# Modulation weights on their own buffers and GpSimd's queue in a hybrid diffusion layer

## The chip, the cores and the metric

The kernel runs on one core of one Trainium2 chip. A core has a matrix engine (TensorE, PE in the profile), a vector engine (VectorE, DVE), an activation engine (ScalarE, ACT), GpSimd (POOL) and SyncE (SP), which here only issues transfers. Sixteen DMA engines move data between the chip's memory (DRAM) and the on-chip buffer. SyncE's transfers form one queue (q1 in the profile), GpSimd's another (q0). The metric is device microseconds of an execution; the time before is the median of three runs.

## What is computed

One layer of a diffusion backbone on 512 latent tokens and 256 context tokens of width 1024, all in float32. Cut to what matters here:

```python
mods = split(silu(c) @ w_mod + b_mod, 9)          # sh1 sc1 g1 sh2 sc2 g2 sh3 sc3 g3, each of 1024
mods_c = split(silu(c_ctx) @ w_mod + b_mod, 9)    # the same for the context tokens
h  = x   + 0.5 * g1  * swiglu(modulate(x,   norm_ffn1, sh1,  sc1),  w_ffn1_in, w_ffn1_out)
hc = ctx + 0.5 * g1c * swiglu(modulate(ctx, norm_ffn1, sh1c, sc1c), w_ffn1_in, w_ffn1_out)
...
h = h + g2 * mixer_output(...)                    # retention and convolution, from h and hc
h = h + 0.5 * g3 * swiglu(modulate(h, norm_ffn2, sh3, sc3), w_ffn2_in, w_ffn2_out)
return rmsnorm(h, final_norm)

def swiglu(x, w_in, w_out):
    a, b = split(x @ w_in, 2)                     # 2 x 2816 columns
    return (silu(a) * b) @ w_out
```

The change lies in the first feed-forward, the two lines with `ffn1`.

## The kernel before

All tensors lie with channels on the 128 partitions and tokens along the row. A float32 product is made of three TensorE products: each operand is split into a rounded part `hi` (a cast on ScalarE) and a rest `lo` (a subtraction on VectorE), and hi x hi, hi x lo and lo x hi are added up in PSUM. So each weight that is loaded goes through DMA, ScalarE and VectorE before TensorE can use it: `unit` (lines 95 to 102) loads into one of four `wraw` buffers through SyncE's queue, casts into one of four `wh` buffers and subtracts into one of four `wl` buffers. `weights` (351 to 357) does the last two steps for weights that are loaded already.

The planner of the language orders the instructions of each engine by their place in the program and by what its model holds to be ready; a load without dependencies may be pulled far forward. Each queue is then served in order. Buffers with one tag are reused in turn, and who needs one waits for its last reader.

`start` (514) loads x and the context, makes the norm and the first shift and scale from the first sixteen blocks of `w_mod` (`first_mods`, 164 to 187, with products on VectorE, ScalarE and, in line 183, GpSimd), and computes two of the 22 column pairs of the feed-forward. At its end it copies x and the context into the DRAM tiles `hdram` and `hcdram` (561, 562).

`ffn1` (424) goes through the 22 column pairs in six groups of 4, 4, 4, 4, 3 and 3 (`GROUPS1`). A group has an input part and an output part. In the first group the pairs 2 and 3 are plain units. All other pairs go through `chunk` (376 to 422), which computes the pair for two quarters of the tokens and weights with seven products in place of eight: `operands` (359) makes sums of tokens once, and `chunk` makes sums of the halves a11, a12, a21, a22 of its weights, into `wy` buffers. Its products are lines 405, 407, 409, 411, 413, 416 and 419 (all matmuls are recorded at line 400), their first Silu is line 410. Its results lie in `sg` buffers.

The output part has four steps (two in the last group and then a tail), each with one load of `w1o` and two blocks of 128 channels for latents (px) and context (pc). For the first five groups `part_sum` (595 to 601) scales each block by its gate on ScalarE into `t` buffers, of which there are six, and adds them to `hdram` and `hcdram` by accumulating stores on GpSimd's queue. The last group loads the sums back (`open_h`, 603 to 613, on SyncE's queue), adds its own block (`evac1`, `evac1c`) and runs the next norm's sums beside it (`tail1`).

Between these parts `mod_step` (568) computes the other 56 blocks of the modulation, in the order of `MOD_STEPS`: `mods` (194 to 204) loads 128 rows of `w_mod` (512 KB) into a `wraw` buffer through SyncE's queue, and VectorE multiplies them by c and, for the first 24, by c_ctx, with the sum kept and the product thrown away into a `t` buffer. Steps 0 to 7 give the gate g1, which `part_sum` needs; it is finished as a whole at step 7. Four steps follow each plain unit, one each chunk and two each output step, until the 56 are used up.

Of the kernel before, what the change touches and what calls it, by code (L numbers as in the profile page):

```python
# [10 lines left out]
F32 = mybir.dt.float32  # L11
# [5 lines left out]
P = 128  # L17
# [7 lines left out]

GROUPS1 = ((0, 4), (4, 4), (8, 4), (12, 4), (16, 3), (19, 3))
LA = L + LC
H = LA // 2
# [24 lines left out]

HOME = {"hx": "right1", "th": "left1", "tl": "left1", "wy": "left1", "sg": "left1"}
HOME.update({t: "left2" for t in ("gx", "gc", "y", "sx", "sc")})
# [4 lines left out]
def hybrid_layer_kernel(ctx: ExitStack, tc: tile.TileContext, a: dict, out: bass.AP):  # L60
# [31 lines left out]
    def raw_tile(shape):  # L92
        return t_(shape, F32, "wraw", 4)
# [100 lines left out]
    def mods(n):  # L194
        i, b = MOD_STEPS[n]
        raw = raw_tile((P, D))
        nc.sync.dma_start(raw, a["w_mod"][n])
        j = 8 * i + b
        for v, dst in ((0, mx), (1, mc)):
            if v == 1 and i > 4:  # L200
                continue
            junk = tmp((P, D), BF16)
            nc.vector.scalar_tensor_tensor(  # L203
                junk, raw, 1.0, ccrow[v], ALU.mult, ALU.mult, accum_out=dst[:, j:j + 1])
# [99 lines left out]
    def part(us, c):  # L304
        return [(hi[:, c], lo[:, c]) for hi, lo in us]
# [53 lines left out]
    def operands(kb):  # L359


        b1, b2 = hx[kb], hx[kb + 4]
        b11, b12, b21, b22 = b1[:, :H], b1[:, H:], b2[:, :H], b2[:, H:]
        ta, tb = t_((P, 2, H), F32, "wy", 2), t_((P, 2, H), F32, "wy", 2)
        nc.vector.tensor_sub(ta[:, 0, :], b11, b12)
        nc.vector.tensor_sub(ta[:, 1, :], b12, b22)
        nc.vector.tensor_sub(tb[:, 0, :], ta[:, 1, :], b11)
        nc.vector.tensor_add(tb[:, 1, :], b21, tb[:, 0, :])
        out = []
        for i, t in enumerate((ta, tb)):  # L370
            hi, lo = t_((P, 2, H), F32R, f"th{2 * kb + i}"), t_((P, 2, H), F32R, f"tl{2 * kb + i}")
            split(hi, lo, t)
            out += [(hi[:, n, :], lo[:, n, :]) for n in range(2)]
        return out

    def chunk(j, u, t):
# [6 lines left out]
        a11, a12, a21, a22 = r0[:, :q], r0[:, q:], r1[:, :q], r1[:, q:]  # L383
        y0, y1 = t_((P, 2, q), F32, "wy", 2), t_((P, 2, q), F32, "wy", 2)
        w0 = weights(r0)
        nc.vector.tensor_add(y0[:, 0, :], a21, a11)
        nc.vector.tensor_add(y0[:, 1, :], a21, a22)
        w1 = weights(y0.rearrange("p a b -> p (a b)"))
        nc.vector.tensor_add(y1[:, 0, :], y0[:, 1, :], a11)
        nc.vector.tensor_add(y1[:, 1, :], y1[:, 0, :], a12)  # L390
        w2 = weights(y1.rearrange("p a b -> p (a b)"))
        w3 = weights(a22)
        lo_, hi_ = slice(0, H), slice(H, LA)
# [9 lines left out]
        p1, p7 = tmp()[:, :H], tmp()[:, :H]  # L403
        s, c = t_((P, LA), F32, "sg", 3), t_((P, LA), F32, "sg", 3)
        product(pa, w0, 0, part(u[:4], lo_), True)
# [4 lines left out]
        nc.scalar.activation(s[:, lo_], pa, AF.Silu)  # L410
        product(pc, w1, 1, [x[0] for x in t], True)
        nc.vector.tensor_sub(p7, p7, pc)
        product(pb, w2, 0, [x[2] for x in t], True)
        nc.vector.tensor_add(p1, p1, pb)
        nc.vector.tensor_sub(c[:, hi_], p7, p1)
        product(pc, w2, 1, part(u[4:], hi_), False)
        nc.vector.tensor_add(s[:, hi_], p1, pc)
        nc.scalar.activation(s[:, hi_], s[:, hi_], AF.Silu)
        product(pd, w3, 0, [x[3] for x in t], False)
        nc.vector.tensor_sub(c[:, lo_], pd, p1)  # L420
        nc.vector.tensor_mul(s, s, c)
        return s

    def ffn1(u):
# [7 lines left out]
        def plain(pa, pb, pc):  # L432
            s = t_((P, LA), F32, "sg", 3)
            nc.scalar.activation(s[:, xs], pa, AF.Silu)
            nc.vector.tensor_mul(s[:, xs], s[:, xs], pb)
            nc.scalar.activation(s[:, cx], pc[:, 0, :], AF.Silu)
            nc.vector.tensor_mul(s[:, cx], s[:, cx], pc[:, 1, :])
            return s
# [6 lines left out]
        off = 0  # L445
        for k0, nk in GROUPS1:
            for j in range(2 if k0 == 0 else 0, nk):
                if k0:
                    keep(j, chunk(k0 + j, u, t))
                    mod_step(1)  # L450
                    continue
                wa, wb = units(a["w1i"][j])
                pa, pb, pc = ps(), ps(), ps((P, 2, LC))
                proj(pa, wa, ux)
                proj(pb, wb, ux)
                proj(pc[:, 0, :], wa, uc)
                proj(pc[:, 1, :], wb, uc)
                keep(j, plain(pa, pb, pc))
                mod_step(4)
            n = 2 * nk * P  # L460
# [8 lines left out]

            for mm in range(2 if last else 4):  # L470
                w = out_units(mm)
                px, pc = [ps() for _ in range(2)], [ps() for _ in range(2)]
# [4 lines left out]
                for i in range(2):  # L477
# [3 lines left out]
                    else:  # L481
                        part_sum(2 * mm + i, px[i], pc[i][:, :LC])
                if not last:
                    mod_step(2)
            if last:
                w = out_units(2) + out_units(3)
                for i in range(4):
                    pc = ps()
                    proj(pc[:, :LC], w[i], gc_)
                    evac1c(hc, 4 + i, pc[:, :LC])  # L490
                mod_step(99)
                px = [ps() for _ in range(4)]
# [21 lines left out]
    def start(u, uc):  # L514
# [45 lines left out]
        nc.gpsimd.dma_start(rope, a["rope"])  # L560
        nc.gpsimd.dma_start(hdram, a["xT"])
        nc.gpsimd.dma_start(hcdram, a["ctxT"])
        return [(px[0], px[1], pc[0]), (px[2], px[3], pc[1])]

    todo = list(range(len(MOD_STEPS)))
    hg = {}

    def mod_step(count):
        for _ in range(count):
            if todo:  # L570
                n = todo.pop(0)
                mods(n)
                if n == 7:
                    hg["x1"] = gate_vec("x1", mx, 2, True)
                    hg["c1"] = gate_vec("c1", mc, 2, True)
                if n == 23:
# [13 lines left out]
    accc = t_((P, LC), F32, "accc")  # L590
    hdram = dp.tile([P, KT, L], F32, name="hdram")

    hcdram = dp.tile([P, KT, LC], F32, name="hcdram")

    def part_sum(b, px, pc):

        r, rc = tmp(), tmp()[:, :LC]
        nc.scalar.activation(r, px, AF.Identity, scale=hg["x1"][:, b:b + 1])
        nc.gpsimd.dma_start(hdram[:, b, :], r, accum_op=ALU.add)
        nc.scalar.activation(rc, pc, AF.Identity, scale=hg["c1"][:, b:b + 1])  # L600
        nc.gpsimd.dma_start(hcdram[:, b, :], rc, accum_op=ALU.add)  # L601

    def open_h():
# [5 lines left out]
        for b in range(KT):  # L609
            nc.sync.dma_start(h[b], hdram[:, b, :])  # L610
        for i in range(4):
            nc.sync.dma_start(hc2[i], hcdram[:, 2 * i:2 * i + 2, :])
        return h, [hc2[b // 2][:, b % 2, :] for b in range(KT)]
# [360 lines left out]
    for b in range(KT):  # L974
        nc.gpsimd.dma_start(h[b], hdram[:, b, :])
    acc = t_((P, L), F32, "acc")
# [164 lines left out]
```

## Time and profile before

| | us |
|---|---|
| median of three runs | 1820.78 (1819.42 to 1824.73) |
| the profiled execution | 1822.34 |
| its span, first to last instruction | 1819.9 |
| TensorE matmuls busy | 1740.2 |
| VectorE busy | 1148.4 |
| ScalarE busy | 673.6 |
| GpSimd busy | 138.3 |
| mean granted clock of TensorE | 0.979 |

The profile records one execution. Its views are the page (busy time of each engine, groups of instructions, the kinds of transfers), windows (busy time of each engine in a stretch that one picks), timelines (instructions of one engine in order: start, length, engine, line, operation, output<-inputs, and in brackets the idle time just before with what ended it) and the DMA view (packets, MB and share of the 16 engines for each queue, in a stretch).

### The profile page before, as it was taken

Reading aid. Unit: us, or ns where it says so; the run is one execution under the profiler, and the core shown is the slowest. Engines: PE = TensorE matmul, PEld = TensorE weight load, DVE = VectorE, ACT = ScalarE, POOL = GpSimd, SP = SyncE. Lnnn points to the kernel's source line nnn. Section 1 sums busy time; section 2 is a strip of 40 time slices with the busy share of each in tenths; the row PEclk is TensorE's granted clock in tenths of the full one; section 3 lists DMA queues with packets and bytes.
Section 4 is the critical chain, followed back from the end, with each engine's and each line's share of the span. In section 5 each row is a group of like instructions: output and inputs, shape, how many; then the busy total and the mean of one; then the engine's idle time right before and its main releaser. Section 6 shows DMA issues by size and latency. Waiting matters only on the chain.

```text
span 1819.9 us, 22626 instructions
## 1 busy us (share of the span) xinstructions
PE 1740.2 (96%) x8918; PEld 1506.7 (83%) x8918; DVE 1148.4 (63%) x1796; ACT 673.6 (37%) x963; POOL 138.3 (8%) x193
## 2 busy tenths in 40 slices
PE   5888999989899789999999999999999999999998
PEld 3677989989899788888888888888888988888887
DVE  5895958566665678877579398474665643333335
ACT  4632434333344532342334234233373332222232
POOL 2303020201121100000000000001010000000000
PEclk8999999999999889999999999999999999999999
DMA  9248475654764513133124115213562233233331
GB/s 325 99 150 180 134 168 169 159 164 125 188 155 94 194 33 104 58 110 122 58 70 168 64 47 174 68 60 128 185 226 99 81 105 93 96 95 99 100 86 46
DMA packets 74062, 221.96 MB, mean 122 GB/s; under 512 B 8818, under 2 KB 14962, under 8 KB 73908
## 3 DMA queue, kind: packets, MB, share of 16 engines
q1 hardware_dynamic: 55444, 179.35, 30.2%
q0 software_dynamic: 17936, 40.13, 9.8%
q8 instruction: 69, 1.13, 0.2%
q10 hardware_dynamic: 576, 1.05, 0.2%
q14 instruction: 37, 0.30, 0.1%
HBM read 192.18 MB, written 31.46 MB: 123 GB/s over the span
## 4 chain that ended last, share of the span: by engine, by line
PE 74%; issue 11%; DVE 6%; DMA 6%; POOL 1%; ACT 1%; DVEq 0%; SPq 0%; POOLq 0%; ACTq 0%
PE ps L108 21%; PE ps L109 21%; PE ps L110 21%; PE ps L400 10%; DMA wraw<-in_w1i 2%; DMA wraw<-in_w1o 1%; DVE wl L101 1%; DMA hx<-in_xT 1%; DVE t L203 1%; DMA wraw<-in_dist_x 1%; DVE h L697 1%; DMA th<-in_w_mod 1%; POOL t L183 1%; POOL hcdram L601 0%; ACT wh L99 0%
## 5 line engine op out<-in xcount | busy, mean ns | idle before, releaser
L99 ACT CAST wh<-wraw 128x1024 fp32r<-128x1024 f32 (+2 forms) x212 | 219.4, 1036 | 557.5 <-PE ps L109 303.9
L101 DVE TENSOR_TENSOR wl<-wraw,wh 128x1024 fp32r<-128x1024 f32 (+2 forms) x212 | 254.3, 1202 | 243.3 <-ACT wh L99 238.2
L108 PE MATMUL ps<-uh,wh 128*128 128x512 f32 (+1 forms) x924 | 333.5, 363 | 8.2 <-ACT wh L99 6.8
L110 PE MATMUL ps<-uh,wl 128*128 128x512 f32 (+1 forms) x924 | 331.6, 360 | 0.9 <-DVE wl L101 0.9
L109 PE MATMUL ps<-ul,wh 128*128 128x512 f32 (+1 forms) x832 | 299.1, 361 | 0.1
L108 PEld LDWEIGHTS ps<-uh,wh 128*128 128x128 f32 x924 | 176.0, 191 | 35.4 <-ACT wh L99 7.2
L109 PE MATMUL ps<-gx,wh 128*128 128x512 f32 (+1 forms) x544 | 204.0, 377 | 0.0
L110 PE MATMUL ps<-gx,wl 128*128 128x512 f32 (+1 forms) x544 | 204.0, 377 | 0.0
L108 PE MATMUL ps<-gx,wh 128*128 128x512 f32 (+1 forms) x544 | 203.7, 377 | 0.2 <-ACT gx L297 0.2
L110 PEld LDWEIGHTS ps<-uh,wl 128*128 128x128 f32 x924 | 175.9, 191 | 27.2 <-DVE wl L101 1.7
L697 DVE SCALAR_TENSOR_TENSOR h<-y,vec,h 128x512 f32<-128x512 f32 x240 | 179.6, 748 | 5.5
L109 PEld LDWEIGHTS ps<-ul,wh 128*128 128x128 f32 x832 | 158.7, 191 | 24.3 <-DVE ul L511 0.9
L108 PE MATMUL ps<-hx,wh 128*128 128x512 f32 (+1 forms) x364 | 124.2, 341 | 10.4 <-DVE gx L587 6.0
L110 PE MATMUL ps<-hx,wl 128*128 128x512 f32 (+1 forms) x364 | 123.6, 340 | 1.1 <-DVE wl L101 1.1
L109 PE MATMUL ps<-hx,wh 128*128 128x512 f32 (+1 forms) x364 | 123.4, 339 | 0.0
L108 PEld LDWEIGHTS ps<-gx,wh 128*128 128x128 f32 x544 | 102.1, 188 | 18.9 <-ACT gx L297 0.4
L110 PEld LDWEIGHTS ps<-gx,wl 128*128 128x128 f32 x544 | 102.0, 188 | 18.8
L109 PEld LDWEIGHTS ps<-gx,wh 128*128 128x128 f32 x544 | 102.0, 188 | 18.7
L400 PE MATMUL ps<-th,wh 128*128 128x384 f32 x288 | 97.5, 339 | 4.0 <-ACT wh L355 3.9
L400 PE MATMUL ps<-tl,wh 128*128 128x384 f32 x288 | 96.5, 335 | 0.0
L400 PE MATMUL ps<-th,wl 128*128 128x384 f32 x288 | 95.8, 335 | 0.0
L108 PEld LDWEIGHTS ps<-hx,wh 128*128 128x128 f32 x364 | 70.6, 194 | 18.9 <-DVE gx L587 6.5
(271 smaller groups left out, 3114.3 us busy)
## 6 DMA issues: line engine op xcount, KB each, us to landing
wraw<-in_w_mod SPq DMA_DIRECT2D x56, 512.0 KB, 4.2
wraw<-in_w1i SPq DMA_DIRECT2D x44, 512.0 KB, 5.7
wraw<-in_w2i SPq DMA_DIRECT2D x44, 512.0 KB, 3.8
hdram<-t POOLq DMA_DIRECT2D x40, 256.0 KB, 6.1
wraw<-in_w1o SPq DMA_DIRECT2D x16, 512.0 KB, 3.8
wraw<-in_w_cv SPq DMA_DIRECT2D x16, 512.0 KB, 3.8
wraw<-in_w_v SPq DMA_DIRECT2D x16, 512.0 KB, 6.0
wraw<-in_w_rg SPq DMA_DIRECT2D x16, 512.0 KB, 3.7
```

The lines of the kernel that those rows point to most:

```text
L99: nc.scalar.copy(hi, raw)
L101: nc.vector.tensor_sub(lo, raw, f32(hi))
L108: nc.tensor.matmul(o, w[0], x[0], start=first, stop=False)
L109: nc.tensor.matmul(o, w[0], x[1], start=False, stop=False)
L110: nc.tensor.matmul(o, w[1], x[0], start=False, stop=last)
L183: nc.gpsimd.tensor_mul(m, raw[1][n], ccrow[1][:, c])
L203: nc.vector.scalar_tensor_tensor(junk, raw, 1.0, ccrow[v], ALU.mult, ALU.mult, accum_out=dst[:, j:j + 1])
L400: nc.tensor.matmul(o, w[i][:, ws], x[k][m], start=first and k == n == 0, stop=k == 3 and n == 2, skip_group_check=True)
L697: nc.vector.scalar_tensor_tensor(o, y[:, t:t + L], vec[:, w0 + t:w0 + t + 1], o, ALU.mult, ALU.add)
```

## The change

`mods` loads into two buffers of its own (`wm`) through GpSimd's queue. The steps are spread by two tables, `STEPS_IN` and `STEPS_OUT`, over the input and output parts of the six groups, and in an output part they stand ahead of a step in place of behind it. The gate g1 is made column by column, each behind its own step. `hcdram` goes: `hdram` has rows of 768, `part_sum` writes latents and context into one `sg` buffer (now four of 768) and adds it with one accumulating store. `open_h` loads through GpSimd's queue, context in turn with latents. `chunk` makes one sum in a `wy` buffer and the other three in place, in the raw weights, and takes the seven products in another order, with the one on a22 in fourth place. `operands` uses `sg` buffers. The scratch of GpSimd's transfers is halved.

```diff
+STEPS_IN = (0, 2, 2, 8, 9, 3)
+STEPS_OUT = (8, 6, 6, 6, 6, 0)
...
     def mods(n):
         i, b = MOD_STEPS[n]
-        raw = raw_tile((P, D))
-        nc.sync.dma_start(raw, a["w_mod"][n])
+        raw = t_((P, D), F32, "wm", 2)
+        nc.gpsimd.dma_start(raw, a["w_mod"][n])
...
-        ta, tb = t_((P, 2, H), F32, "wy", 2), t_((P, 2, H), F32, "wy", 2)
+        ta, tb = t_((P, 2, H), F32, "sg", 4), t_((P, 2, H), F32, "sg", 4)
...
-        y0, y1 = t_((P, 2, q), F32, "wy", 2), t_((P, 2, q), F32, "wy", 2)
+        y = t_((P, q), F32, "wy")
         w0 = weights(r0)
-        nc.vector.tensor_add(y0[:, 0, :], a21, a11)
-        nc.vector.tensor_add(y0[:, 1, :], a21, a22)
-        w1 = weights(y0.rearrange("p a b -> p (a b)"))
-        nc.vector.tensor_add(y1[:, 0, :], y0[:, 1, :], a11)
-        nc.vector.tensor_add(y1[:, 1, :], y1[:, 0, :], a12)
-        w2 = weights(y1.rearrange("p a b -> p (a b)"))
-        w3 = weights(a22)
+        nc.vector.tensor_add(y, a21, a22)
+        nc.vector.tensor_add(a21, a21, a11)
+        w1 = weights(r1)
+        w2 = weights(y)
+        nc.vector.tensor_add(a11, y, a11)
+        nc.vector.tensor_add(a12, a11, a12)
+        w3 = weights(r0)
...
         product(pa, w0, 1, part(u[4:], lo_), False)
         nc.scalar.activation(s[:, lo_], pa, AF.Silu)
-        product(pc, w1, 1, [x[0] for x in t], True)
+        product(pd, w1, 1, [x[3] for x in t], False)
+        product(pc, w2, 0, [x[0] for x in t], True)
         nc.vector.tensor_sub(p7, p7, pc)
-        product(pb, w2, 0, [x[2] for x in t], True)
+        product(pb, w3, 0, [x[2] for x in t], True)
         nc.vector.tensor_add(p1, p1, pb)
+        product(pc, w3, 1, part(u[4:], hi_), False)
         nc.vector.tensor_sub(c[:, hi_], p7, p1)
-        product(pc, w2, 1, part(u[4:], hi_), False)
+        nc.vector.tensor_sub(c[:, lo_], pd, p1)
         nc.vector.tensor_add(s[:, hi_], p1, pc)
         nc.scalar.activation(s[:, hi_], s[:, hi_], AF.Silu)
-        product(pd, w3, 0, [x[3] for x in t], False)
-        nc.vector.tensor_sub(c[:, lo_], pd, p1)
         nc.vector.tensor_mul(s, s, c)
...
-                    mod_step(1)
+                    mod_step(STEPS_IN[gi] * (j + 1) // nk - STEPS_IN[gi] * j // nk)
...
-                mod_step(4)
...
             for mm in range(2 if last else 4):
+                mod_step(STEPS_OUT[gi] * (mm + 1) // 4 - STEPS_OUT[gi] * mm // 4)
                 w = out_units(mm)
...
-                if not last:
-                    mod_step(2)
...
-        nc.gpsimd.dma_start(hdram, a["xT"])
-        nc.gpsimd.dma_start(hcdram, a["ctxT"])
+        nc.gpsimd.dma_start(hdram[:, :, xs], a["xT"])
+        nc.gpsimd.dma_start(hdram[:, :, cx], a["ctxT"])
...
-                if n == 7:
-                    hg["x1"] = gate_vec("x1", mx, 2, True)
-                    hg["c1"] = gate_vec("c1", mc, 2, True)
+                if n < 8:
+                    for key, src in (("x1", mx), ("c1", mc)):
+                        nc.vector.tensor_scalar(hg[key][:, n:n + 1], src[:, 16 + n:17 + n],
+                                                vec[:, V_BM + 16 + n:V_BM + 17 + n], 0.5, ALU.add, ALU.mult)
...
-    hdram = dp.tile([P, KT, L], F32, name="hdram")
-    hcdram = dp.tile([P, KT, LC], F32, name="hcdram")
+    hdram = dp.tile([P, KT, LA], F32, name="hdram")
...
-        r, rc = tmp(), tmp()[:, :LC]
-        nc.scalar.activation(r, px, AF.Identity, scale=hg["x1"][:, b:b + 1])
+        r = t_((P, LA), F32, "sg", 4)
+        nc.scalar.activation(r[:, xs], px, AF.Identity, scale=hg["x1"][:, b:b + 1])
+        nc.scalar.activation(r[:, cx], pc, AF.Identity, scale=hg["c1"][:, b:b + 1])
         nc.gpsimd.dma_start(hdram[:, b, :], r, accum_op=ALU.add)
-        nc.scalar.activation(rc, pc, AF.Identity, scale=hg["c1"][:, b:b + 1])
-        nc.gpsimd.dma_start(hcdram[:, b, :], rc, accum_op=ALU.add)
...
         for b in range(KT):
-            nc.sync.dma_start(h[b], hdram[:, b, :])
-        for i in range(4):
-            nc.sync.dma_start(hc2[i], hcdram[:, 2 * i:2 * i + 2, :])
+            nc.gpsimd.dma_start(h[b], hdram[:, b, xs])
+            if b % 2 == 1:
+                nc.gpsimd.dma_start(hc2[b // 2], hdram[:, b - 1:b + 1, cx])
...
-    nc = _bacc.Bacc("TRN2", target_bir_lowering=False, num_devices=1, dynamic_dma_scratch_size=8192)
+    nc = _bacc.Bacc("TRN2", target_bir_lowering=False, num_devices=1, dynamic_dma_scratch_size=4096)
```

More of the change, by code (lines that the diff above doesn't have):

```diff
@@ L50 @@
 )
-HOME = {"hx": "right1", "th": "left1", "tl": "left1", "wy": "left1", "sg": "left1"}
+HOME = {"hx": "right1", "th": "left1", "tl": "left1", "wy": "left1", "sg": "left1", "wm": "left1"}
 HOME.update({t: "left2" for t in ("gx", "gc", "y", "sx", "sc")})
@@ L403, in chunk @@
         p1, p7 = tmp()[:, :H], tmp()[:, :H]
-        s, c = t_((P, LA), F32, "sg", 3), t_((P, LA), F32, "sg", 3)
+        s, c = t_((P, LA), F32, "sg", 4), t_((P, LA), F32, "sg", 4)
         product(pa, w0, 0, part(u[:4], lo_), True)
@@ L432, in plain @@
         def plain(pa, pb, pc):
-            s = t_((P, LA), F32, "sg", 3)
+            s = t_((P, LA), F32, "sg", 4)
             nc.scalar.activation(s[:, xs], pa, AF.Silu)
@@ L445, in ffn1 @@
         off = 0
-        for k0, nk in GROUPS1:
+        for gi, (k0, nk) in enumerate(GROUPS1):
             for j in range(2 if k0 == 0 else 0, nk):
@@ L490, in ffn1 @@
                     evac1c(hc, 4 + i, pc[:, :LC])
-                mod_step(99)
                 px = [ps() for _ in range(4)]
@@ L560, in start @@
         nc.gpsimd.dma_start(rope, a["rope"])
-        nc.gpsimd.dma_start(hdram, a["xT"])
-        nc.gpsimd.dma_start(hcdram, a["ctxT"])
+        nc.gpsimd.dma_start(hdram[:, :, xs], a["xT"])
+        nc.gpsimd.dma_start(hdram[:, :, cx], a["ctxT"])
         return [(px[0], px[1], pc[0]), (px[2], px[3], pc[1])]
     todo = list(range(len(MOD_STEPS)))
-    hg = {}
+    hg = {key: cp.tile([P, 8], F32, name=f"g_{key}") for key in ("x1", "c1")}
     def mod_step(count):
@@ L974, in hybrid_layer_kernel @@
     for b in range(KT):
-        nc.gpsimd.dma_start(h[b], hdram[:, b, :])
+        nc.gpsimd.dma_start(h[b], hdram[:, b, xs])
     acc = t_((P, L), F32, "acc")
```

## The prediction

> **What bounds the kernel now.** I read the page first (its engines), next the windows view with borders set on evacuations of ScalarE, then the timelines of the queues at one gap, then the DMA view.
>
> ```profile
> PE 1740.2 (96%) x8918; PEld 1506.7 (83%) x8918; DVE 1148.4 (63%) x1796; ACT 673.6 (37%) x963; POOL 138.3 (8%) x193
> ```
>
> TensorE is the bound. It stands idle for some 80 us of the 1820; what the change can win must be in such gaps. It touches the first feed-forward (about 94 to 640 us), so I cut that into stages. Row: from:to and length, PE, PEld, DVE, ACT, POOL busy with counts, granted clock, DMA share, GB/s.
>
> ```profile
> 93.70:110.56 16.86, 16.86 (x99) 14.96 (x98) 16.51 (x28) 7.22 (x11) 0.00 (x0) 1.00 0.20 63
> 110.56:136.12 25.56, 18.71 (x97) 15.87 (x96) 22.13 (x38) 4.96 (x7) 0.00 (x0) 0.87 0.63 206
> 136.12:183.48 47.36, 41.02 (x216) 34.22 (x214) 26.16 (x42) 14.12 (x23) 14.08 (x16) 0.96 0.83 179
> 183.48:203.44 19.96, 18.73 (x104) 18.00 (x105) 18.60 (x26) 8.98 (x14) 0.00 (x0) 1.00 0.44 146
> 217.65:232.21 14.56, 14.56 (x86) 14.56 (x85) 12.49 (x20) 6.28 (x10) 0.00 (x0) 1.00 0.34 111
> 232.21:285.87 53.66, 50.56 (x274) 44.22 (x273) 32.80 (x64) 20.68 (x33) 14.52 (x17) 0.97 0.80 191
> 285.87:301.16 15.29, 15.29 (x90) 15.29 (x89) 14.48 (x23) 7.63 (x12) 0.00 (x0) 1.00 0.50 155
> 330.27:385.14 54.87, 52.62 (x295) 46.76 (x294) 26.35 (x37) 19.24 (x30) 13.80 (x16) 1.00 0.84 202
> 357.52:365.94 8.42, 8.42 (x51) 7.33 (x50) 3.51 (x5) 3.38 (x5) 3.43 (x4) 1.00 1.08 275
> 385.14:402.80 17.66, 14.41 (x69) 14.09 (x68) 13.61 (x20) 6.39 (x10) 0.00 (x0) 0.81 0.24 83
> 431.92:486.88 54.96, 52.93 (x296) 46.82 (x294) 26.86 (x40) 19.23 (x30) 13.83 (x16) 1.00 0.84 202
> 486.88:502.63 15.75, 13.15 (x67) 13.08 (x67) 13.60 (x20) 6.29 (x10) 0.00 (x0) 0.89 0.26 93
> 516.98:557.15 40.17, 40.17 (x231) 36.89 (x230) 19.55 (x27) 18.58 (x30) 13.91 (x16) 1.00 0.82 175
> 557.15:571.71 14.56, 14.56 (x86) 14.56 (x85) 11.00 (x15) 6.29 (x10) 0.00 (x0) 1.00 0.21 55
> ```
>
> Undisturbed, a seven-product chunk takes 14.56 us (217.65, 557.15), an output step (two blocks) 8.42, four of them 33.68, a plain unit 16.86. The border "first Silu of a chunk" (line 410) lies three of seven products into it. So the stage from the last such border of a group to the first of the next should take 14.56 + 33.68 = 48.24; with three chunks a group, 14.56 + 25.26 = 39.82. What is over: second plain unit 25.56 - 16.86 = 8.70; first output part 47.36 - 33.68 - 6.24 = 7.44, the chunk after it 19.96 - 14.56 = 5.40; next groups 5.42 + 0.73, 6.63 + 3.10, 6.72 + 1.19; the last one 0.35. Sum **45.7 us**, idle time and the slowed clock after it together (0.81 in the row at 385.14).
>
> The last row but one is the key. In 516.98:557.15 the same accumulating stores run, DMA share 0.82, and only 0.35 us is lost. What is missing there is the modulation loads: the loop counters (8, 8, 4, 8, 4, 8, 4, 8, 3, then 1) have used up all 56. At a gap with them:
>
> ```profile
> 376.00 0.33 SPq L197 DMA_DIRECT2D wraw<-in_w_mod  x1
> ...
> 378.26 0.33 SPq L381 DMA_DIRECT2D wraw<-in_w1i  x1
> ...
> 386.44 0.69 DVE L386 TENSOR_TENSOR wy<-wraw,wraw 128x512 f32<-128x512 f32 x1 [4.19 <-DMA wraw<-in_w1i]
> ...
> 388.79 0.69 PE L400 MATMUL ps<-uh,wh 128*128 128x384 f32 x1 [3.25 <-DVE t L412]
> ...
> 148.49 1.23 DVE L203 SCALAR_TENSOR_TENSOR t<-wraw,kl 128x1024 bf16<-128x1024 f32 x1 [6.24 <-DMA hdram<-t]
> ```
>
> SyncE's queue is served in order and all its loads share four `wraw` buffers. The modulation load at 376.00 waits for a buffer, the chunk's weights stand behind it, VectorE waits 4.19 us for them, and TensorE 3.25 us for VectorE. The buffer was late because the modulation product writes its junk to a `t` buffer that an accumulating store still reads (6.24 us at 148.49).
>
> **The change, part by part.** Everything is reckoned against the profiled execution, 1822.34 us (span 1819.9 and 2.4 around it), 1.56 above the median 1820.78; I carry the difference over.
>
> *Own buffers and queue for modulation.* SyncE and `wraw` lose 56 loads; POOL gets them. Behind a waiting load on POOL now stand the accumulating stores, and for those wait their `sg` buffers, ScalarE's evacuations and at last PSUM. Four buffers give a block four times 4.21 us, 16.8, before its buffer is needed again.
>
> ```profile
> q1 hardware_dynamic: 2163, 7.89, 44.3%
> q0 software_dynamic: 2304, 3.15, 38.9%
> ...
> L203 DVE SCALAR_TENSOR_TENSOR t<-wraw,kh 128x1024 bf16<-128x1024 f32 x56 | 67.6, 1219 | 2.9 <-DMA hdram<-t 2.2 <-DMA hcdram<-t 0.7
> L203 DVE DVE_READ_ACCUMULATOR t<-wraw,kh 128x1 f32 x56 | 4.6, 82 | 0.0
> wraw<-in_w_mod SPq DMA_DIRECT2D x56, 512.0 KB, 4.2
> ```
>
> These two queue rows are those of 330.27:385.14. Plain loads: 7.89 MB in 44.3% of 54.87 us is 24.3 us of the 16 engines, 325 GB/s, so 1.61 us for 524 KB. Accumulating: 38.9% is 21.3 us for eight pairs, 2.67 each. An output part of groups 1 to 3 asks now for 21.3 + 8 x 1.61 + 4 x 1.61 + (2 to 4) x 1.61 = 43.8 to 47.1 us of engines in 33.7: full, hence the stalls. After: six modulation loads, so 40.6 to 43.8 at most. One store of 384 KB in place of 256 + 128 isn't in the trace: its cost lies between 1.34 (half, if descriptors set it) and 2.67 (bytes); I take 2.67, as both sizes move whole rows, which makes -10.7 us of engines per part the favourable end. Still over 33.7, but now the excess is modulation data on a queue that no product waits for, and chunk weights are issued early, since `wraw` serves them alone. I put what is left at 1.5 us for each of groups 1 to 3, between 0.35 and the 3.2 that two loads fewer leave certain to go.
>
> *Order of steps* (0/8, 2/6, 2/6, 8/6, 9/6, 3/0 for input/output part). The second plain unit has no modulation ahead of it: 8.70 to 0. The first output part has eight, with the gates of block b made from step b just ahead of its evacuation: I leave 4.0 of 12.8 (ends 0 and 12.8). The gates become 16 instructions on one column instead of four; VectorE is busy 3.51 of 8.42 us in a step, which hides them. In groups 3 and 4 VectorE gets 4 x 11.00 + 8 x 1.30 = 54.4 in 58.2 us and 3 x 11.00 + 9 x 1.30 = 44.7 in 43.7 (11.00 from 557.15; 1.30 is 1.219 and 0.082 for its accumulator read): 1.0 too much, I count it. The last output part gets six loads: 0.35 becomes 1.5.
>
> *Sums in place, new product order.* As many additions, casts and products; raw weights stay in their buffers longer, which the four buffers without modulation cover. The last product now feeds a Silu ahead of the multiply; the output part starts with the other chunks' products, which hide it. 0; without the cover some 0.5 us a group, 3.
>
> *Loads of h on POOL.*
>
> ```profile
> 593.42 3.24 SPq L97 DMA_DIRECT2D wraw<-in_w_q  x2
> 596.76 4.27 SPq L610 DMA_DIRECT2D gx<-hdram  x8
> 601.12 0.75 DVE L587 SCALAR_TENSOR_TENSOR gx<-ps,g_x,gx 128x512 f32<-128x512 f32 x1 [3.83 <-DMA gx<-hdram]
> 615.57 0.38 PE L108 MATMUL ps<-hx,wh 128*128 128x256 f32 x1 [3.79 <-DVE gx L587]
> ```
>
> They come now behind SyncE's next weights (593.42), context blocks last; TensorE's 3.79 us at 615.57 wait for these evacuations. Issued from POOL, context in turn with latents, they should start some us earlier: -3 (ends -6, the stall and what clock it costs, and +2 if POOL is late). Behind it the norm's chain is late next, unchanged.
>
> *Start.*
>
> ```profile
> q0 software_dynamic: 45, 1.97, 127.9%
> q1 hardware_dynamic: 46, 0.09, 7.4%
> ...
> 3.28 0.53 POOL L561 DMA_DIRECT2D hdram<-in_xT  x1
> 3.31 3.81 SPq L517 DMA_DIRECT2D hx<-in_xT  x7
> 17.82 2.69 ACT L242 ACTIVATE t<-hx 128x512 f32<-128x512 f32 x4 [1.13 <-DMA hx<-in_xT]
> ```
>
> The queue rows are from 8 to 12 us: the copies of x and context into `hdram` move 1.97 MB in 45 packets, some 44 KB each, while x itself, which everything awaits (ScalarE until 17.82), gets 0.09 MB in 46. With rows of 2 and 1 KB in the new layout the copy may crowd x less (-4 at best); but the first two modulation loads will be pulled up here as the copies were, 2 x 1.61 = 3.2 us of engines, and POOL may wait ahead of line 183 (+4). I take 0. The Trainium skill, "DMA: Bandwidth & Descriptors", section "Queues, rings and completion order", says that an engine takes a packet from each ring in turn, and these rows agree (45 and 46 packets). By that rule the 2.1 MB of x would get half of 325 GB/s and land 12.9 us after 3.3, 1.6 us sooner than the 17.8 of now, and the sum would be 1781.5.
>
> *Sum.* Left over: 0 + 4.0 + 3 x 1.5 + 1.0 + 1.5 = 11.0 of 45.7, so -34.7; -3; 0: **-37.7**, 1784.6 for a profiled execution, **1783** as the median.
>
> **Rivals.**
>
> *The DMA engines stay the bound.* For it: 43.8 to 47.1 us asked of 33.7, and 40.6 to 43.8 after. Then only the second unit's 8.7 and two loads in each of groups 1 to 3, 9.7, go: 1802. Against it: 516.98:557.15, share 0.82 with 0.35 lost. The Trainium skill, same page, section "Issuing engines are not separate DMA queues", says that all issuing engines' transfers run on the same 16 and that a second one saves issue time only. By that rule alone this rival's time would hold; but the rows at 376.00 show waits for buffers, not for engines. 0.18.
>
> *VectorE becomes the bound in groups 3 and 4*, as its queue is served in order and each modulation product may wait for its load: 17 x 1.30 = 22 us exposed, 1805. Against it: 217.65:232.21 holds 14.56 with a modulation product for both vectors in it. 0.07.
>
> *Slower: POOL convoys the start.* Modulation load n waits for VectorE's products of n - 2; if the planner puts such loads between line 183's products, each of the eight first blocks waits for one turn: 4.2 to land and two products of 1.30, 6.8 us, eight times 54: 1837. It decides from 4.7 us a block (37.7 / 8). For it: the copies went out at 3.3 us, far ahead of their place in the program. Against it: modulation products aren't mixed into the blocks now, though there are gaps. 0.06.
>
> *It doesn't do what it says*: the wait for a free buffer just moves from SyncE to POOL and comes back through `sg` and PSUM: 1820. Against it stands the 16.8 us of slack. 0.05.
>
> **How the numbers follow.** Forecast 0.64. Its own ends: 3 us left of the 45.7, -5.7 and -4 give 1769; the slow ends of its terms overlap with the first two rivals. The range 1769 to 1805 takes these in and leaves the last two cases out, with a little of the forecast's own edges. Faster by over 0.3% (about 5.5 us, what a measurement here can tell from no change): 0.64 + 0.18 + 0.07 = 0.89; same 0.05; slower 0.06.
>
> **What would show it.** Right: the stages of all groups near 48.2 (39.8) us and 14.6 for the chunk after them, no `in_w1i` wait on VectorE or ScalarE, clock 1.00 in between, the second unit near 16.9. Wrong: `wh` casts waiting for DMA in output parts (first rival); VectorE full in 380 to 500 us and line 400 waiting for it (second); POOL waiting ahead of line 183, and the plain unit starting well after 94 us (third); ScalarE's scaled evacuations waiting for stores (fourth).

## The result, and the profile after

The changed kernel takes 1777.05 us (median of four runs, 1775.26 to 1779.33), the kernel before 1822.72 in the same comparison (1819.42 to 1824.73). The ratio is 0.9752, with a 95% interval of 0.9730 to 0.9774: 2.5% faster. The profiled execution took 1775.92 us, its span is 1774.1, 45.8 shorter than before; the mean granted clock is 0.987, before 0.979.

The engines' row of the page, changed kernel (busy time, share of the span, instructions):

```profile
PE 1720.5 (97%) x8918; PEld 1495.8 (84%) x8918; DVE 1148.9 (65%) x1808; ACT 674.4 (38%) x963; POOL 141.9 (8%) x221
```

As many matmuls are busy for 19.7 us less, and TensorE idles 26.1 us less. Some 14 of the 19.7 are clock, an estimate from the two mean clocks (0.008 of 1740 us). The windows view of the changed kernel, cut where the prediction cut (the first Silu of a chunk is line 414 now), same columns:

```profile
112.68:129.34 16.66, 16.66 (x98) 14.77 (x97) 16.49 (x36) 3.82 (x7) 2.71 (x5) 1.00 0.63 214
129.34:169.27 39.93, 39.93 (x231) 35.74 (x230) 18.15 (x30) 15.58 (x27) 8.60 (x11) 1.00 0.84 183
169.27:183.83 14.56, 14.56 (x86) 14.56 (x85) 13.14 (x18) 6.39 (x11) 0.00 (x0) 1.00 0.23 80
212.95:261.31 48.36, 48.36 (x278) 43.88 (x277) 30.74 (x47) 19.05 (x30) 10.88 (x15) 1.00 0.82 205
305.00:354.77 49.77, 49.77 (x286) 45.29 (x285) 36.76 (x73) 21.57 (x35) 12.50 (x18) 1.00 0.78 192
354.77:367.92 13.15, 13.15 (x78) 13.15 (x77) 11.98 (x17) 6.32 (x9) 0.38 (x1) 1.00 0.55 195
397.05:446.85 49.80, 48.84 (x278) 43.97 (x277) 26.71 (x40) 19.36 (x31) 11.88 (x17) 1.00 0.83 209
446.85:461.84 14.99, 14.86 (x86) 14.54 (x85) 13.95 (x20) 6.50 (x11) 0.83 (x2) 1.00 0.49 165
476.22:521.50 45.28, 41.83 (x231) 37.98 (x230) 26.17 (x42) 18.39 (x31) 12.15 (x18) 0.96 0.89 230
```

The second plain unit and the first output part lose nothing, the next two groups 0.1 us each (48.36 against 48.24, and 49.77 + 13.15 against 48.24 + 14.56: there the Silu alone came late, behind an ACT_TABLE_LOAD of ScalarE that took 1.28 us at 353.5), the fourth border 1.6 + 0.4. The last row, the stage into the last group, should be 39.82: it loses 5.5, and this loss is new (0.35 before).

How the 45.8 us divide can be read from the first and last start of that Silu (view of one line's instructions: shortest, middle and longest in ns, first and last start). Before:

```profile
L410 ACT ACTIVATE sg<-ps x18: 477/482/493, 183.5 to 586.1; 128x384 f32<-128x384 f32 x18
```

and after:

```profile
L414 ACT ACTIVATE sg<-ps x18: 473/482/494, 169.3 to 550.4; 128x384 f32<-128x384 f32 x18
```

Up to the first: -14.2 us; between first and last: 402.6 to 381.1, -21.5; from the last to the end: 1233.8 to 1223.7, -10.1.

### The profile page after: what moved, and what is told of

Read it like the earlier page. It is cut to its first block, busy times and chain, and to the rows that moved or that the text cites. A ratio compares the mean times of both kernels' runs of the same rounds, so it can differ in the third digit from the quotient of the medians.

```text
span 1774.1 us, 22474 instructions
## 1 busy us (share of the span) xinstructions
PE 1720.5 (97%) x8918; PEld 1495.8 (84%) x8918; DVE 1148.9 (65%) x1808; ACT 674.4 (38%) x963; POOL 141.9 (8%) x221
## 5 line engine op out<-in xcount | busy, mean ns | idle before, releaser
L113 PEld LDWEIGHTS ps<-uh,wl 128*128 128x128 f32 x924 | 175.1, 190 | 26.7 <-DVE wl L104 1.3
L111 PE MATMUL ps<-hx,wh 128*128 128x512 f32 (+1 forms) x364 | 121.5, 336 | 5.3 <-ACT hx L300 3.8
L112 PE MATMUL ps<-hx,wh 128*128 128x512 f32 (+1 forms) x364 | 121.7, 334 | 0.7 <-DVE hx L301 0.7
L359 DVE TENSOR_TENSOR wl<-wraw,wh 128x1024 fp32r<-128x1024 f32 x54 | 66.1, 1223 | 55.6 <-ACT wh L358 55.4
```

The costliest lines, as they stand in the source:

```text
L111: nc.tensor.matmul(o, w[0], x[0], start=first, stop=False)
L112: nc.tensor.matmul(o, w[0], x[1], start=False, stop=False)
L113: nc.tensor.matmul(o, w[1], x[0], start=False, stop=last)
L359: nc.vector.tensor_sub(lo, src, f32(hi))
```

## The experiments

There are twelve more kernels. Each was timed against the kernel before on its own chip; the ratio is the figure to compare, and its interval is about 0.002 to 0.004 to either side. A cost in microseconds below is a difference of medians; where the ratios give another, both are named. "First", "between" and "tail" are the three stretches above, from each profiled execution. The tail is the least steady: in the ten kernels that load h on GpSimd's queue it goes from 1223.7 to 1232.3 us, though most of their edits lie ahead of it.

| kernel | median us | before | ratio | first | between | tail |
|---|---|---|---|---|---|---|
| before | 1822.72 | | 1 | 183.5 | 402.6 | 1233.8 |
| changed | 1777.05 | 1822.72 | 0.9752 | 169.3 | 381.1 | 1223.7 |
| e1: modulation on SyncE's queue | 1775.25 | 1821.88 | 0.9753 | 168.2 | 378.2 | 1224.6 |
| e2: shared `wraw` buffers | 1781.66 | 1821.88 | 0.9787 | 168.1 | 387.4 | 1227.1 |
| e9: e1 and e2 | 1782.76 | 1818.96 | 0.9794 | 168.4 | 383.0 | 1229.5 |
| e3: old places of the steps | 1787.40 | 1821.88 | 0.9827 | 172.1 | 388.2 | 1225.7 |
| e5: two stores, from `t` buffers | 1795.49 | 1821.88 | 0.9872 | 173.6 | 391.2 | 1228.1 |
| e8: two stores, from `sg` | 1778.30 | 1822.40 | 0.9762 | 169.3 | 381.7 | 1232.3 |
| e4: loads of h on SyncE's queue | 1785.78 | 1822.40 | 0.9792 | 168.8 | 379.6 | 1231.1 |
| e6: steps spread otherwise | 1780.06 | 1822.40 | 0.9771 | 168.6 | 381.9 | 1224.9 |
| e7: copies on SyncE's queue | 1773.01 | 1822.40 | 0.9727 | 161.2 | 381.8 | 1227.7 |
| b1: before, stores from `sg` | 1788.21 | 1818.96 | 0.9819 | 178.3 | 373.9 | 1236.0 |
| b2: before, sums in place | 1817.60 | 1818.96 | 0.9992 | 184.9 | 399.1 | 1231.9 |
| c1: e1 and e7 | 1761.26 | 1818.96 | 0.9674 | 157.4 | 375.9 | 1227.2 |

### Was it the queue or the shared buffers? (e1, e2, e9)

e1 issues the modulation loads from SyncE again; e2 puts them into the four `wraw` buffers again; e9 does both.

```diff
-        nc.gpsimd.dma_start(raw, a["w_mod"][n])      # e1, e9
+        nc.sync.dma_start(raw, a["w_mod"][n])
-        raw = t_((P, D), F32, "wm", 2)               # e2, e9
+        raw = raw_tile((P, D))
```

> The changed kernel with the modulation loads back on SyncE's queue, still in their own two buffers. Theory (it was the queue: a load that waits for its buffer stands ahead of a chunk's weights): groups 1 to 3 lose some 3 us each again and the time rises by 8 to 15 us, to 1785 to 1792, with waits of VectorE and ScalarE for in_w1i loads. Rival (it was the shared buffers; the queue is of no account): within 3 us of 1777. A second rival: the 7 us still lost around group 4 came from modulation loads standing behind the accumulating stores on GpSimd's queue; on SyncE's queue they do not, so the time falls to about 1770.

> The changed kernel with the modulation loads on GpSimd's queue but in the four wraw buffers again. Theory (buffers): a chunk's weights wait for a buffer whose modulation product waits for a load behind the accumulating stores, so the cost is larger than in the kernel before: 1795 to 1825. Rival (the queue alone did it): within 3 us of 1777.

> The changed kernel with the modulation loads both on SyncE's queue and in the shared wraw buffers, as before; stores, schedule, sums and loads of h stay changed. Theory (with the t buffers free, a modulation load on the weights' queue and buffers is soon used and costs little): 1775 to 1783. Rival (the prediction's mechanism, a modulation load that waits for its buffer with a chunk's weights behind it, is worth some 3 us for each of groups 1 to 3 and more in groups 3 and 4): 1788 or more.

e1: 0.9753 against 0.9752. The queue gave nothing that the time shows, and the theory fell: over all borders e1's stages lose 4.4 us, the changed kernel's 7.3. Nor did the second rival's 1770 come, though the stage into the last group does lose less (below). e2 costs 4.6 us by the medians (6.4 by the ratios), below the range expected of it. e9, with both undone, costs 5.7 (7.7): by the median it stands at the upper end of the theory's range, by the ratio (1785) between that range and the rival's 1788. So in the changed kernel, what the prediction took for the mechanism is worth 6 to 8 us of some 45. What own buffers and queue would have given alone in the kernel before, with the stores still reading `t` buffers, was not run.

### The `t` buffers (e5, e8, b1)

e5 puts two stores a block from `t` buffers back into the changed kernel; e8 makes two stores as well, but both from the one `sg` buffer.

```diff
-        r = t_((P, LA), F32, "sg", 4)                # e5
-        nc.scalar.activation(r[:, xs], px, AF.Identity, scale=hg["x1"][:, b:b + 1])
+        r, rc = tmp(), tmp()[:, :LC]
+        nc.scalar.activation(r, px, AF.Identity, scale=hg["x1"][:, b:b + 1])
+        nc.gpsimd.dma_start(hdram[:, b, xs], r, accum_op=ALU.add)
...
-        nc.gpsimd.dma_start(hdram[:, b, :], r, accum_op=ALU.add)
+        nc.gpsimd.dma_start(hdram[:, b, cx], rc, accum_op=ALU.add)
```

```diff
-        nc.gpsimd.dma_start(hdram[:, b, :], r, accum_op=ALU.add)          # e8
+        nc.gpsimd.dma_start(hdram[:, b, xs], r[:, xs], accum_op=ALU.add)
...
+        nc.gpsimd.dma_start(hdram[:, b, cx], r[:, cx], accum_op=ALU.add)
```

> The changed kernel with two accumulating stores a block again, from t buffers, as before (same DRAM layout). Theory (the t buffers held by stores are what made VectorE's modulation products late): waits of these products for hdram stores come back and the time rises by 5 to 15 us. Rival (own buffers and queue for the loads are enough): within 2 us, with only some 0.3 us more of the 16 engines for each block.

> The changed kernel with two accumulating stores a block, both from the one sg buffer (e5 had them from t buffers, and cost 18 us). Theory (what cost in e5 were the t buffers, which VectorE's modulation products and other work need while a store reads them): within 4 us of 1777. Rival (it is the number of stores: GpSimd issues 40 more at about 1.1 us and the 16 engines carry more packets): 1790 to 1796 as in e5.

e5 costs 18.4 us (21.9 by the ratios), the most of all parts undone and more than the 5 to 15 expected, and e8 costs 1.3 (its runs reach from 1775.24 to 1785.31, the profiled one being the longest): it isn't the number of stores, it is which buffers they read from. Two groups of instructions of e5 (busy time, mean ns | idle time before them and what ended it) show who waits for a store:

```profile
L598 ACT ACTIVATE t<-ps,g_x 128x512 f32<-128x512 f32 x40 | 27.6, 689 | 67.2 <-PE ps L113 31.7 <-DMA hdram<-t 27.2 <-DVE t L206 5.8
...
L206 DVE SCALAR_TENSOR_TENSOR t<-wm,kl 128x1024 bf16<-128x1024 f32 x24 | 29.3, 1220 | 10.7 <-DMA hdram<-t 9.8 <-ACT t L598 0.9
```

ScalarE's evacuations wait 27.2 us, and VectorE's products 9.8, for stores that still read the `t` buffer next in turn. So b1 takes the kernel before and lets the stores read `sg` buffers. With this come a fourth `sg` buffer and the halved scratch space, as in the change:

```diff
-        r, rc = tmp(), tmp()[:, :LC]
+        r = t_((P, LA), F32, "sg", 4)
+        r, rc = r[:, xs], r[:, cx]
```

> The kernel before with one thing changed: each block's two accumulating stores read an sg buffer (four of them in place of three) and no t buffers; modulation loads, their queue and buffers, the steps, the sums and the loads of h stay as before. Theory (it was the t buffers, held by stores, that stopped VectorE's junk products and ScalarE's evacuations; undoing this part in e5 cost 18 us, undoing the queue in e1 nothing): the time falls by 12 to 25 us, to 1797 to 1810, and the waits of VectorE's modulation products for hdram stores are gone. Rival (the prediction's: the modulation loads in SyncE's queue and in wraw buffers hold the weights up whatever the products wait for): less than 6 us, above 1815.

1788.21 against 1818.96: **30.8 us** (32.9 by the ratio) from this edit, more than the theory asked. In the changed kernel the fourth buffer and the scratch space are not what counts: e5 has both and still takes 17.2 us more than e8, from which it differs only in where the stores read. In the kernel before, the two were not changed alone. The windows of b1, same cut (line 410):

```profile
111.14:137.54 26.40, 19.67 (x97) 16.52 (x96) 25.76 (x45) 4.97 (x7) 0.00 (x0) 0.81 0.65 212
137.54:178.34 40.80, 40.80 (x234) 36.45 (x233) 30.54 (x45) 17.36 (x28) 14.03 (x16) 1.00 0.97 244
...
313.95:362.24 48.29, 48.29 (x278) 43.92 (x277) 27.07 (x39) 19.15 (x30) 13.87 (x16) 1.00 0.95 237
362.24:376.80 14.56, 14.56 (x86) 14.56 (x85) 12.13 (x17) 6.39 (x10) 0.00 (x0) 1.00 0.24 80
405.93:454.21 48.28, 48.28 (x278) 43.92 (x277) 27.31 (x42) 19.15 (x30) 13.86 (x16) 1.00 0.93 234
454.21:468.77 14.56, 14.56 (x86) 14.56 (x85) 12.14 (x17) 6.38 (x10) 0.00 (x0) 1.00 0.25 85
```

Every group runs undisturbed (0.05 us over in 313.95:362.24, where the kernel before lost 6.63), although the modulation loads still go through SyncE's queue and the `wraw` buffers, in the old places. The first output part takes 0.9 longer (40.80 against 39.92) with TensorE busy throughout. Only the second plain unit keeps its loss (26.40 against 16.86). How six `t` buffers could cost so much is seen in the order of work. Some of SyncE's loads and of VectorE's work in the kernel before, in the stage that starts at 330.27:

```profile
343.60 9.92 SPq L197 DMA_DIRECT2D wraw<-in_w_mod  x2
...
355.49 7.23 SPq L197 DMA_DIRECT2D wraw<-in_w_mod  x2
363.53 0.33 SPq L380 DMA_DIRECT2D wraw<-in_w1i  x1
364.67 0.33 SPq L381 DMA_DIRECT2D wraw<-in_w1i  x1
```

```profile
353.09 1.22 DVE L203 SCALAR_TENSOR_TENSOR t<-wraw,kh 128x1024 bf16<-128x1024 f32 x1
...
362.28 1.22 DVE L203 SCALAR_TENSOR_TENSOR t<-wraw,kh 128x1024 bf16<-128x1024 f32 x1
...
372.06 1.23 DVE L356 TENSOR_TENSOR wl<-wraw,wh 128x1024 fp32r<-128x1024 f32 x1 [7.41 <-ACT wh L355]
```

and in b1, in the stage that starts at 313.95:

```profile
327.87 0.33 SPq L380 DMA_DIRECT2D wraw<-in_w1i  x1
329.00 0.33 SPq L381 DMA_DIRECT2D wraw<-in_w1i  x1
```

```profile
330.04 1.22 DVE L203 SCALAR_TENSOR_TENSOR t<-wraw,kh 128x1024 bf16<-128x1024 f32 x1
...
334.79 1.23 DVE L356 TENSOR_TENSOR wl<-wraw,wh 128x1024 fp32r<-128x1024 f32 x1 [3.53 <-ACT wh L355]
```

So I read it: an output step takes six `t` buffers, four for its two blocks, two for the junk of its two modulation products. With six in all, each product needs the buffer of a store one step back, so the products are placed between the steps and paced by the stores; they hold their `wraw` buffers meanwhile, and the chunk's weights are loaded 34.4 us into the stage (364.67 - 330.27). With the stores reading elsewhere, the products are done early and the weights are loaded at 15.1 us (329.00 - 313.95), 19 us sooner. In the first two output parts of the kernel before, VectorE and ScalarE do wait for stores, 35.7 us between 136 and 290 us; in this stage neither shows such a wait. What the stores set here, on this reading, is the order of work, and it shows as a wait for weights. That the stores' use of the `t` buffers is the cause is shown by b1; how the order comes about is read from these rows and shown by no run.

### The places of the steps (e3, e6)

e3 puts them back (4 behind a plain unit, 1 behind a chunk, 2 behind an output step); e6 spreads them.

```diff
-                    mod_step(STEPS_IN[gi] * (j + 1) // nk - STEPS_IN[gi] * j // nk)      # e3
+                    mod_step(1)
...
+                mod_step(4)
...
-                mod_step(STEPS_OUT[gi] * (mm + 1) // 4 - STEPS_OUT[gi] * mm // 4)
...
+                if not last:
+                    mod_step(2)
```

```diff
-STEPS_IN = (0, 2, 2, 8, 9, 3)
-STEPS_OUT = (8, 6, 6, 6, 6, 0)
+STEPS_IN = (0, 4, 4, 8, 6, 6)                        # e6
+STEPS_OUT = (8, 5, 5, 5, 5, 0)
```

> The changed kernel with the modulation steps where they stood before (four behind each plain unit, one behind each chunk, two behind each output step). Theory (the order of steps is worth what the prediction put on it): the second plain unit loses 8.7 us again and each output part of groups 1 to 3 has two loads more, some 3 us each; group 4, with 4 steps in place of 15, gives back its 7: 1785 to 1790. Rival (with own buffers and queue the place of the steps hardly matters, but nine steps in three chunks do): 1768 to 1774, faster than the changed kernel.

> The changed kernel with the steps spread as 0/8, 4/5, 4/5, 8/5, 6/5, 6/0 (input/output part of the six groups). Theory (the 7 us left over come from nine steps in the three chunks of group 4 and six in its output part, whose loads stand behind the accumulating stores): the stage into the last group loses 1 to 2 us in place of 5.46 and the time falls to 1770 to 1774. Rival (VectorE has no room: groups 1 and 2 now carry two-vector products in every chunk, 11.0 + 2.6 of 14.56 us, and group 5 six in three chunks): the loss moves there and the time is 1775 to 1782.

e3 is 10.4 us slower (13.7 by the ratios). The time is near what the theory gave, but not all of its parts are. The second plain unit loses 2.5 us and not 8.7 (19.38 against 16.86). The chunk after the first border loses 4.3, the stages of groups 1 to 3 with the chunk behind 1.5, 4.2 and 3.9. The stage into the last group gives back 4.6 of its 5.5. But b1 has the same places and loses nothing in its groups, so e3's losses need something else of the change as well. The loads on GpSimd's queue, where they stand among the accumulating stores, are the likely one: VectorE waits 8.1 us for modulation loads between 298 and 366 us of e3, and 6.5 us in all between 100 and 560 us of b1. No run differs from e3 in the queue alone. The theory of e6 fell: the stage into the last group lost 6.55 us, not 1 to 2, with fewer steps there. The rival's time (1775 to 1782) holds 1780.06, but its reason doesn't: the loss stayed where it was. What tells the runs apart is the queue. With the new places and the loads on GpSimd's queue that stage lost 5.46 (changed), 5.60 (e2), 3.76 (e4), 6.74 (e5), 6.55 (e6), 6.16 (e7) and 5.61 (e8); on SyncE's queue 1.49 (e1), 1.54 (e9) and 1.21 (c1). The stage in e1:

```profile
476.15:517.46 41.31, 40.42 (x231) 36.81 (x230) 25.83 (x42) 17.95 (x31) 6.87 (x8) 1.00 0.96 260
```

The timelines of the changed kernel show the chain:

```profile
484.70 1.23 DVE L206 SCALAR_TENSOR_TENSOR t<-wm,kh 128x1024 bf16<-128x1024 f32 x1 [3.50 <-DMA wm<-in_w_mod]
```

```profile
488.93 0.52 ACT L424 ACTIVATE sg<-sg 128x384 f32<-128x384 f32 x1 [4.30 <-DVE sg L423]
```

```profile
491.83 1.65 PE L111 MATMUL ps<-hx,wh 128*128 128x512 f32 x4 [3.45 <-ACT hx L300]
```

VectorE waits for a modulation load with the last chunk's work (423) queued behind it, ScalarE for VectorE, TensorE for ScalarE. This load was issued at 477.13 and took 7.5 us to land, the one before it 3.5. GpSimd had issued no accumulating store since 441.42, so it didn't stand behind one; why it was late stays open. e1's own median shows only 1.8 us of this, which its interval can't tell from nothing.

### The loads of h and the start (e4, e7)

```diff
-            nc.gpsimd.dma_start(h[b], hdram[:, b, xs])      # e4; the context's loads likewise, after it
+            nc.sync.dma_start(h[b], hdram[:, b, xs])
-        nc.gpsimd.dma_start(hdram[:, :, xs], a["xT"])       # e7; the context's copy likewise
+        nc.sync.dma_start(hdram[:, :, xs], a["xT"])
```

> The changed kernel with the loads of h and the context sums in the last group back on SyncE's queue, context behind latents. Theory (their place on GpSimd's queue gave the 9.0 us by which the tail behind the last chunk is shorter, three times the forecast): TensorE's stall of 3.8 us behind these evacuations comes back and the time rises by 6 to 9 us, to 1783 to 1786. Rival (the tail is shorter because the accumulating stores and SyncE's own loads are done sooner; the queue does little): within 2 us of 1777.

> The changed kernel with the two copies of x and the context into hdram issued on SyncE's queue at the end of the start, in place of GpSimd's, where they are pulled up to 3 us. Theory (the 2.1 us by which the first plain unit ends later come from these copies taking engine time from x): ScalarE is done with x at 18 us or sooner in place of 20.9 and the time falls by 2 to 5 us, to 1772 to 1775. Rival (behind x they stand in front of the first modulation blocks and the weights on SyncE's queue): the start gets 2 to 6 us longer, 1779 to 1783.

e4 costs 8.7 us, as its theory said (7.3 by the ratios, whose intervals just overlap). Its tail is 7.4 longer, which alone would not tell it from the spread of the tails. The windows around the norm behind the last group, changed kernel:

```profile
550.40:580.40 30.00, 28.52 (x184) 26.49 (x183) 22.01 (x38) 16.39 (x28) 10.23 (x21) 1.00 0.71 246
580.40:610.40 30.00, 23.83 (x182) 23.11 (x181) 25.48 (x72) 15.87 (x30) 3.79 (x7) 0.89 0.37 123
610.40:640.40 30.00, 24.34 (x162) 22.14 (x162) 24.01 (x40) 9.89 (x16) 0.00 (x0) 0.89 0.08 21
640.40:670.40 30.00, 30.00 (x146) 25.34 (x145) 23.36 (x32) 7.94 (x9) 0.00 (x0) 1.00 0.29 103
```

and e4:

```profile
548.45:578.45 30.00, 27.17 (x171) 24.99 (x169) 20.24 (x33) 14.31 (x24) 2.97 (x9) 1.00 0.67 229
578.45:608.45 30.00, 21.73 (x134) 20.94 (x134) 23.86 (x69) 15.89 (x30) 3.77 (x7) 0.72 0.42 139
608.45:638.45 30.00, 24.67 (x197) 23.64 (x195) 20.52 (x41) 11.24 (x20) 0.00 (x0) 0.97 0.01 1
638.45:668.45 30.00, 29.67 (x137) 25.06 (x138) 23.64 (x31) 7.72 (x10) 0.00 (x0) 0.92 0.36 115
```

Over the four windows TensorE idles 16.8 us in e4 and 13.3 in the changed kernel, and the granted clocks add up to 3.61 and 3.78 of four: 3.5 us by idle time and 0.17 of 30 us, some 5, by clock. In these two executions the clock cost more than the idle time. The idle time is the stall that the theory named: TensorE waits 5.1 us for these evacuations (line 589) in e4, 1.6 in the changed kernel. The other profiled executions agree: in the 120 us behind the last such Silu, TensorE is busy 102.8 to 105.0 us at a clock of 0.89 to 0.90 in the four kernels with these loads on SyncE's queue (before, b1, b2, e4), and 104.7 to 107.7 us at 0.91 to 0.94 in the ten others.

e7 gains 4.0 us, as its theory said. ScalarE's last wait for a block of x, changed kernel and then e7:

```profile
20.89 0.63 ACT L245 ACTIVATE t<-hx 128x512 f32<-128x512 f32 x1 [1.91 <-DMA hx<-in_xT]
```

```profile
11.86 1.81 ACT L245 ACTIVATE t<-hx 128x512 f32<-128x512 f32 x3 [1.46 <-DMA hx<-in_xT]
```

In the kernel before, this wait ended at 17.82. The first Silu of e7 is 8.1 us sooner, but the tail 4.0 longer; nothing in the edit touches the tail.

### Sums in place, and both kernels beaten (b2, c1)

b2 is the kernel before with `chunk`'s additions and products as in the change (the lines of its diff from `y = t_(...)` to the last product), nothing else; c1 is the changed kernel with e1's and e7's edits.

> The kernel before with only the weight sums in place and the other order of the seven products. Theory (worth nothing by itself, since as many additions, casts and products run): within 3 us of 1822. Rival (raw weights that stay in wraw buffers longer hold up SyncE's queue, which modulation loads share here): 1825 to 1832.

> The changed kernel with the modulation loads on SyncE's queue in their own buffers (e1) and the copies into hdram on SyncE's queue at the end of the start (e7). Theory (both gains add: e7's 4 us at the start, e1's 4 us at the stage into the last group): 1768 to 1772, faster than both kernels. Rival (the two share SyncE's queue, the copies then stand before the first modulation loads and weights, or the tail gives it back): 1773 to 1777.

b2: 0.9992, interval 0.9976 to 1.0009, as the theory said: nothing. (The sums weren't undone in the changed kernel.) c1: 1761.26 us, 0.9674 (0.9660 to 0.9689), **faster than both kernels** and by more than the two gains, below the 1768 to 1772 expected. c1 differs from e7 by the queue of the modulation loads alone, and that is worth 9.7 us by the ratios, though e1 showed nothing against the changed kernel: the first Silu comes 3.7 us sooner, the stages take 5.9 us less (5.0 of it the stage into the last group) and the tail 0.5. At the start, with neither copies nor modulation loads on the other queue, SyncE's loads have the engines alone. Queues from 8 to 12 us (packets, MB, share of the 16 engines), changed kernel, then e7, then c1:

```profile
q0 software_dynamic: 267, 1.09, 69.6%
q1 hardware_dynamic: 268, 0.50, 33.0%
```

```profile
q1 hardware_dynamic: 539, 0.98, 67.2%
q0 software_dynamic: 151, 0.54, 33.3%
```

```profile
q1 hardware_dynamic: 770, 1.41, 102.0%
```

## Why the prediction was right, and where it wasn't

The forecast was -37.7 us for a profiled execution, and -46.4 was measured (1822.34 to 1775.92); as the median 1783 was forecast and 1777.05 measured. The sum stood because it counted what TensorE lost, whatever the cause, and the change removed several causes at once. The cause that the prediction named was not the main one. That the time came out within the range all the same was luck: the edit that counted most, the store from `sg`, stood in the sum with no gain, and the changed kernel without it (e5), for which the sum would be the same 1783, takes 1795.49.

- **"What is missing there is the modulation loads."** The stage 516.98:557.15 lost 0.35 us with all stores running, and the prediction put that down to the loads, their queue and their `wraw` buffers. What was missing too, but for one product at 530.78, were the products and the junk that they write. b1 keeps the loads where they were and loses 0.05 in such a stage. e1 has the queue back at no cost, e9 queue and buffers for 6 to 8 us. This step failed. So did the reading of the gap: the load at 376.00 waited 10.9 us for line 390, the weight sums of the chunk ahead, not for a modulation product, and the row at 148.49 is of the first output part; between 290 and 390 us neither VectorE nor ScalarE waits for a store. The prediction had the true link in hand (6.24 us at 148.49, a `t` buffer still read by a store) but used it only to say why a `wraw` buffer was late, and gave the edit that cuts it, the store from `sg`, no gain but engine time.
- **The DMA budget** (43.8 to 47.1 us of engines asked in 33.7). The need was right: b1's stage has 0.95 of 48.29, 45.9 us. The time set against it was wrong: loads run ahead into the input part and stores land in it, so the whole stage of 48.24 counts. Only 0.05 us was lost at 0.95. This also ends the rival that the DMA engines stay the bound (1802). The Trainium skill, "DMA: Bandwidth & Descriptors", section "Issuing engines are not separate DMA queues", says that transfers of all issuing engines run on the same 16; it held as far as e1 shows, where the other issuing engine alone gave nothing (0.9753 against 0.9752), and c1, with fewer transfers on the second queue, was faster than e7.
- **One store for two**: taken at 2.67 us, no gain. It took 2.33 us of the 16 engines in e1's stage 211.84:260.20, where GpSimd's queue moved the eight stores alone (38.6% of 48.36 us). e8 agrees that it matters little: 1.3 us for going back to two.
- **What is left of the 45.7**: 11.0 was forecast and 7.7 measured, but elsewhere. The second unit lost 0 as forecast (16.66), the first output part 0 and not 4.0. The stages of groups 1 to 3, the chunk behind included, lost 0.1, 0.1 and 2.0, not 1.5 each. The stage into the last group lost 5.5, not 1.5: the prediction saw six loads and VectorE's 1.0, not that GpSimd's queue would make VectorE wait for them.
- **Loads of h on GpSimd**: the mechanism was right (e4) and the size too small: -3 was forecast with -6 as an end, and undoing them costs 8.7 (7.3 by the ratios). The tail measured -10.1, but tails differ by 8.6 us among kernels that all have these loads on GpSimd's queue. The term counted the stall and little of the clock behind it.
- **Start at 0**: the first plain unit ended 2.1 us later (112.68 against 110.56), within the ends of -4 and +4. e7, without the copies there, has it end at 104.59, so they do hold the start up. The Trainium skill, "DMA: Bandwidth & Descriptors", section "Queues, rings and completion order", gave turns by packet, and 267 to 268 packets in 4 us bear it out. What failed is the half of the bandwidth that the prediction made of it: GpSimd's packets (the copies and one modulation load) are 4.1 KB, SyncE's 1.9 (1.09 and 0.50 MB), so the turns gave 69.6% and 33.0% of the engines, and the last wait for x ended 3.1 us later and not 1.6 sooner.
- **The low end, 1769**: its parts (3 us left of the 45.7, -5.7 and -4) add up to 1768.4 on the median, and -5.7 is not the -6 that the term gives as its end. Nothing hangs on it.
- **The signs of being right**: in the changed kernel neither VectorE nor ScalarE waits for `in_w1i` loads in the groups, as forecast. But that sign doesn't tell the mechanism: b1 shows 36.4 us of such waits between 150 and 560 us, and its groups lose nothing.
- **VectorE as the bound**, **GpSimd convoying the start**, **nothing gained**: none came. VectorE is busy 26.7 of 49.8 us and 26.2 of 45.3 in the stages of groups 3 and 4 to their borders; two modulation loads alone were pulled in among the first blocks (issued at 4.81 and 29.05 us), with no convoy behind them.

## What to carry to other kernels

Look at which ring of buffers a discarded result is written to: when a slow store reads from the same ring, the stores can set the pace of everything written there, and the trace may show it far away, here as weights that are loaded late. Reckon DMA need against the whole stage that loads and stores can spread over, not the part that issues them. When a stretch without a loss is taken as evidence, list all that is missing in it, and undo one part at a time before naming the cause.

## What the runs showed of the hardware

- With the 16 engines at a share of 0.93 to 0.97 for 40 to 48 us, TensorE was busy throughout at a clock of 1.00 (b1's windows).
- Of two queues with work, served packet by packet (267 and 268), the one with packets of twice the size took twice the engines' time (69.6% and 33.0%). Without the copies on that queue (e7) the last wait for x ended at 11.86 us and not 20.89.
- 3.5 us more of idle time within 120 us went with some 5 us more lost by a lower granted clock (changed kernel and e4, one execution each); over the fourteen profiled kernels the clock there is 0.89 to 0.90 at 102.8 to 105.0 us busy and 0.91 to 0.94 at 104.7 to 107.7.
